# Every third low part of U on GpSimd, and 56 gather steps beside the early keys instead of 44

## The chip, the core and the metric

The kernel runs on one core of a Trainium2 chip. Five engines work side by side, each through its own list of instructions in order: TensorE (PE; matrix products, with its weight loads shown as PEld), VectorE (DVE), ScalarE (ACT), GpSimd (POOL) and SyncE (SP, which here only issues DMAs). They wait for each other through semaphores. The metric is the time of one execution on the device, in microseconds (us). Shorter is better.

## The reference

One transformer layer on 512 tokens of width 2048, in float32. It has a mixer (an mLSTM and a forgetting attention, both behind gates), an attention to a memory of 256 rows, and a feed-forward part called PEER; a residual and a layer norm follow each. Only PEER matters here:

```python
sc = einsum('bshpd,hpnd->bshpn', q, sub_keys)        # scores against 2 x 128 keys, 8 heads
top_s, top_i = top_k(sc, 16)                         # of each half
cand = top_s[..., 0, :, None] + top_s[..., 1, None, :]
best_s, best_pos = top_k(cand, 16)                   # 16 of 256 pairs
g = softmax(best_s)                                  # idx: expert number = key0 * 128 + key1
a = einsum('tkd,td->tk', expert_u[idx], x)           # 128 chosen experts per token
out = einsum('tk,tkd->td', gelu(a) * g, expert_v[idx])
```

There are 16384 experts, rows of the tables U and V of 2048 numbers each.

## The kernel before

Every product of the kernel is made to near float32 precision out of three products of rounded parts: a weight block `raw` of 128 x 1024 is loaded by SP, ScalarE writes its rounded high part `whi` (line 134, in `split`), and the low part `wlo`, the rest, is a subtraction: on VectorE (line 137) or, when `split` is called with `pool=True`, on GpSimd (line 136). `load_w` does this for one block; it counts blocks in `work["n"]` and gives every `work["share"]`-th one's low part to GpSimd, none where `share` is 0. Up to the end of the PEER selection `share` is 8; from there on it is 0. `load_w` also keeps in `work["last"]` the last low part that VectorE made.

PEER is computed in two ways. For 288 of the 512 tokens it is dense: TensorE multiplies these tokens with all of U (`stage_a`, one key of 128 experts at a time, two blocks of 128 x 1024 each, called half keys here: 24 matmuls per block), ScalarE takes the gelu (line 1275), the result is multiplied by gates that are zero where an expert was not chosen (`stage_h`, line 1305), split again into `hph` and `hpl`, and multiplied with V (`stage_o`). For the others, the first block of 128 tokens and 64 + 32 tokens of the last block, the chosen rows are gathered: GpSimd issues an indirect DMA of 128 rows (`gather_rows`, line 885; 1 MB each), and VectorE uses them, for U with a dot product (line 913), for V with a multiply-add (line 916). A gather and its use are one step of a generator (`gathered`). Gathered rows have three buffers, and a gather as well as its use waits for `work["last"]`, which paces it. The last block's generators are called `jobs` and have 194 steps.

The stretch that the change touches goes so. First the selection: `select` finds the top 16 for two heads at a time on VectorE (lines 791 to 828), with two kinds of products on GpSimd (`cand`, line 812, and `eq`, line 827); it ends with the two reductions `sel_i` (line 828). The last block is selected first, since its gathers wait for it, then the two blocks that are dense. Then the gates: for 48 tokens at a time, TensorE transposes what was selected (line 1225), VectorE builds one-hot matrices (`o1`, line 1234, and `o0`, line 1240), TensorE multiplies them (line 1242), ScalarE copies the product to `stage` (line 1245) and its queue writes it to memory as `gd` (line 1247). Then `stage_a` for the first `LOOK` = 76 keys, with `EARLY` = 44 steps of `jobs` spread over them. Their gelus are parked in memory (`gad`, line 1277). Then the main loop: V in groups of 8 keys, four column groups each, with the remaining keys of U and the remaining steps of `jobs` in between; `fetch` reads `gd` back (line 1287) and `gad` (line 1291) through the SP queue.

This is the order in the program text. The order on each engine is made by the tile framework when the program is built: it walks a timeline of estimated costs and issues what comes first, so that keys of U, selection and gate building are interleaved, and any change of an operation's engine moves the order of all engines behind it. Once built, it is fixed.

Buffers of the weight blocks come in two rings that take turns: `W` with 3 raw, 2 high and 2 low buffers, and `E` with 3 of each.

Of the kernel before, what the change touches and what calls it, by code (L numbers as in the profile page):

```python
# [46 lines left out]
def build(tc, I, out):  # L47
    nc = tc.nc
    with ExitStack() as ctx:
# [94 lines left out]
        def load_raw(src, n=1024):  # L144
# [7 lines left out]
        work = {"jobs": None, "rate": 0.0, "due": 0.0, "n": 0, "share": 0, "last": None, "hold": False,  # L152
                "quiet": 0, "normed": None}
# [1099 lines left out]
        acc = mn.tile([P, NK, NDENSE], F32, tag="acc", name="acc")  # L1253

        LOOK = 76
        EARLY = 44
        GA_N = 3
        J = 8
        gas, hs, gates = {}, {}, [None]
# [3 lines left out]
        def stage_a(c):  # L1263

            bank = sm_bank()[:, :NDENSE]
            for kt in range(2):
                uh, ul = load_w(I["uT"][c, kt])
                todo = []
                for kk in range(8):
                    sl = slice(kk * P, (kk + 1) * P)  # L1270
                    xh, xl = X2[kt * 8 + kk]
                    todo.append((bank, uh[:, sl], ul[:, sl], xh[:, :NDENSE], xl[:, :NDENSE], kt * 8 + kk, True))
                products(todo, 0, 15)
            ga = gap.tile([P, NDENSE], F32, tag="ga", bufs=GA_N, name=nm("ga"))
            nc.scalar.activation(ga, bank, AF.Gelu)
            if c in spilled:
                nc.scalar.dma_start(gad[c], ga)
            else:
                gas[c] = ga
# [79 lines left out]
        ahead = [min(NC_, LOOK + -(-c * (NC_ - LOOK) // (NC_ - J))) for c in range(NC_)]  # L1359
        spilled = {a for c in range(NC_) for a in range(ahead[c - 1] if c else 0, ahead[c]) if a - c >= GA_N - 1}  # L1360
        njobs, done = sum(2 * n + 1 for _, n in GATHERED), 0
        for a in range(ahead[0]):
            stage_a(a)
            while done * LOOK < a * EARLY:
                next(jobs, None)
                done += 1

        turn_g = [0]
        for c0 in range(0, NC_, J):
            def fill(i, c0=c0):  # L1370
                if i % 2:
                    c = c0 + i // 2
                    while turn_g[0] < njobs - EARLY and turn_g[0] * (NC_ - 16) <= c * (njobs - EARLY):
                        next(jobs, None)
# [82 lines left out]
```

## Time and profile before

| | |
|---|---|
| median of 3 runs | 4901.81 us (4898.5 to 4901.84) |
| the profiled execution | 4913.27 us, span 4911.5 us |
| TensorE busy | 4713.5 us, 96% of the span |
| VectorE | 3736.2 us, 76% |
| ScalarE | 2127.7 us, 43% |
| GpSimd | 1351.3 us, 28% |

The profile is of one execution. A group of instructions is named by its line, engine, operation and the tiles it writes and reads (`wlo<-raw,whi`). Windows give each engine's busy time between two times of the span, with the clock that TensorE was granted (1.00 is full speed). A row of the waits names the waiting engine and line, then who ended the wait. Matmuls overlap, so their mean durations add up to more than their time.

### The profile page before, as it was taken

The numbers are of one execution on the slowest core, as the hardware profiler recorded it, in microseconds if no ns is written. First come the engines' busy times: TensorE is split into PE (matmuls) and PEld (weight loads), VectorE is DVE, ScalarE is ACT, GpSimd is POOL, SyncE is SP. The second block draws the span as 40 slices with busy tenths as digits, with TensorE's granted clock in tenths as the row PEclk, the third lists the DMA queues.
The fourth block names the chain that finished last, engine by engine and source line by source line (L and its number), as shares of the span: only waits on it lengthen the run. The fifth ranks groups of instructions, "written<-read, shape, count | busy, mean of one in ns | idle before, by whom it ended". The sixth has DMA issues, their size and how long they took to land. (4 is left out here: it accounts for less than half of the span.)

```text
span 4911.5 us, 75235 instructions
## 1 busy us (share of the span) xinstructions
PE 4713.5 (96%) x28705; PEld 4353.5 (89%) x28705; DVE 3736.2 (76%) x5363; ACT 2127.7 (43%) x3106; POOL 1351.3 (28%) x1055
## 2 busy tenths in 40 slices
PE   7999999999999999999999999999998999999997
PEld 6888788878888899999988779999998999999997
DVE  7765666665688776888768585899876878888886
ACT  6665666555543322343332334434443433343333
POOL 1122222311124443334444232332001222221211
PEclk9999999999999999999999999999999999999999
DMA  7888898866559899988889575678778999999994
GB/s 249 283 273 282 302 318 311 276 227 207 190 186 356 328 358 341 339 332 328 303 304 379 201 283 171 215 263 278 277 283 320 346 348 342 344 335 349 359 345 146
DMA packets 380027, 1433.60 MB, mean 292 GB/s; under 512 B 43853, under 2 KB 104909, under 8 KB 320625
## 3 DMA queue, kind: packets, MB, share of 16 engines
q1 hardware_dynamic: 266208, 831.34, 48.5%
q0 software_dynamic: 91712, 559.45, 30.4%
q10 hardware_dynamic: 21744, 38.02, 2.1%
q8 instruction: 224, 3.67, 0.3%
q14 instruction: 139, 1.13, 0.1%
HBM read 1339.13 MB, written 89.40 MB: 291 GB/s over the span
## 5 line engine op out<-in xcount | busy, mean ns | idle before, releaser
L134 ACT CAST whi<-raw 128x1024 fp32r<-128x1024 f32 x1472 | 1526.1, 1051 | 1775.3 <-PE mm L208 814.5
L137 DVE TENSOR_TENSOR wlo<-raw,whi 128x1024 fp32r<-128x1024 f32 x1352 | 1695.5, 1265 | 751.8 <-ACT whi L134 556.0
L885 POOL DMA_INDIRECT rows<-in_peer_v,eid x224 | 379.6, 1695 | 815.0 <-DVE xacc L916 431.4
L885 POOL DMA_INDIRECT rows<-in_peer_u,eid x224 | 322.2, 1438 | 1009.4 <-DVE rows L913 357.8
L208 PE MATMUL po<-hph,whi 128*128 128x288 f32 x2048 | 554.3, 298 | 27.8 <-ACT hph L134 16.9
L913 DVE SCALAR_TENSOR_TENSOR rows<-rows,xacc 128x2048 f32<-128x2048 f32 x224 | 525.7, 2351 | 64.2 <-DMA rows<-in_peer_u,eid 63.4
L916 DVE SCALAR_TENSOR_TENSOR xacc<-rows,dots,xacc 128x2048 f32<-128x2048 f32 x224 | 542.0, 2420 | 40.2 <-DMA rows<-in_peer_v,eid 38.9
L208 PE MATMUL sm<-Ch,whi 128*128 128x288 f32 x2048 | 562.2, 299 | 3.5 <-ACT whi L134 2.5
L208 PE MATMUL sm<-Cl,whi 128*128 128x288 f32 x2048 | 560.7, 298 | 0.0
L208 PE MATMUL po<-hpl,whi 128*128 128x288 f32 x2048 | 553.8, 297 | 1.8 <-DVE hpl L137 1.8
L136 POOL TENSOR_TENSOR wlo<-raw,whi 128x1024 fp32r<-128x1024 f32 x120 | 307.9, 2566 | 699.3 <-ACT whi L134 335.7
L208 PE MATMUL mm<-xh,whi 128*128 128x384 f32 x1280 | 437.3, 344 | 8.0 <-ACT whi L134 2.8
L208 PE MATMUL mm<-xl,whi 128*128 128x384 f32 x1280 | 429.4, 337 | 0.0
L208 PEld LDWEIGHTS po<-hph,whi 128*128 128x128 f32 x2048 | 386.0, 190 | 30.6 <-ACT hph L134 17.2
L208 PEld LDWEIGHTS sm<-Ch,whi 128*128 128x128 f32 x2048 | 386.8, 189 | 5.5 <-ACT whi L134 3.0
L208 PEld LDWEIGHTS po<-hpl,whi 128*128 128x128 f32 x2048 | 386.1, 190 | 2.8 <-DVE hpl L137 2.0
L208 PEld LDWEIGHTS sm<-Cl,whi 128*128 128x128 f32 x2048 | 387.2, 189 | 0.0
L208 PE MATMUL po<-hph,wlo 128*128 128x288 f32 x2048 | 340.9, 297 | 1.4 <-DVE wlo L137 1.3
L208 PE MATMUL sm<-Ch,wlo 128*128 128x288 f32 x2048 | 319.2, 297 | 3.1 <-DVE wlo L137 3.1
L208 PEld LDWEIGHTS po<-hph,wlo 128*128 128x128 f32 x2048 | 296.4, 189 | 5.1 <-DVE wlo L137 2.6
L208 PEld LDWEIGHTS sm<-Ch,wlo 128*128 128x128 f32 x2048 | 287.8, 189 | 5.9 <-DVE wlo L137 4.2
L208 PEld LDWEIGHTS mm<-xh,whi 128*128 128x128 f32 x1280 | 241.4, 189 | 16.1 <-issue 4.1
(430 smaller groups left out, 8833.6 us busy)
## 6 DMA issues: line engine op xcount, KB each, us to landing
raw<-in_w_in SPq DMA_DIRECT2D x512, 512.0 KB, 5.6
raw<-in_uT SPq DMA_DIRECT2D x256, 512.0 KB, 5.1
raw<-in_vq SPq DMA_DIRECT2D x256, 512.0 KB, 6.4
raw<-in_w_xkv SPq DMA_DIRECT2D x64, 512.0 KB, 5.3
raw<-in_w_br_ml SPq DMA_DIRECT2D x64, 512.0 KB, 5.2
raw<-in_w_br_fx SPq DMA_DIRECT2D x64, 512.0 KB, 5.8
raw<-in_w_out SPq DMA_DIRECT2D x64, 512.0 KB, 4.4
raw<-in_peer_wq SPq DMA_DIRECT2D x64, 512.0 KB, 3.4
```

What stands on the lines that cost most here:

```text
L134: nc.scalar.copy(hi, src)
L136: return nc.gpsimd.tensor_sub(lo, src, hi.bitcast(F32))
L137: return nc.vector.tensor_sub(lo, src, hi.bitcast(F32))
L208: nc.tensor.matmul(o, w if stat else x, x if stat else w, start=k == first and x is xh and not part, stop=k == last and part == 1)
L885: i = nc.gpsimd.indirect_dma_start(out=rows, out_offset=None, in_=I[table], in_offset=bass.IndirectOffsetOnAxis(ap=ei[:, k:k + 1], axis=0))
L913: after(nc.vector.scalar_tensor_tensor(rows, rows, 1.0, xacc, op0=ALU.mult, op1=ALU.mult, accum_out=dots[:, k:k + 1]), last())
L916: after(nc.vector.scalar_tensor_tensor(xacc, rows, dots[:, k:k + 1], xacc, op0=ALU.mult, op1=ALU.add), last())
```

## The change

While the first `LOOK` keys of U are run ahead, `work["share"]` is 3: every third low part of U is subtracted by GpSimd instead of VectorE, 50 in the whole program. After them it is 0 again, as it was. And `EARLY` is 56: of the 194 gather steps of the last block, 56 are spread over these keys and 138 are left for the main loop, where it was 44 and 150. Nothing else is edited, and the computed values do not depend on it; the order that is built from it differs on all engines.

```diff
-        EARLY = 44
+        EARLY = 56
...
+        work["share"] = 3
         for a in range(ahead[0]):
             stage_a(a)
             while done * LOOK < a * EARLY:
                 next(jobs, None)
                 done += 1
+        work["share"] = 0
```

## The prediction

> **What bounds the kernel now.** I read the busy shares first, then the stage of the change in windows, then who TensorE waited for, and last the prices of the operations that move. The page's first line:
>
> ```profile
> PE 4713.5 (96%) x28705; PEld 4353.5 (89%) x28705; DVE 3736.2 (76%) x5363; ACT 2127.7 (43%) x3106; POOL 1351.3 (28%) x1055
> ```
>
> TensorE is the bound over the whole span; the change acts only after 3105 us. To place the stages I took the first and last starts (the last two times of each row) of three kinds of matmul: products of U (`sm`), gate-building products (`po<-o,o`), products with V (`po<-hph`).
>
> ```profile
> L208 PE MATMUL sm<-Ch,whi x2048: 289/295/445, 3105.1 to 4813.3; 128*128 128x288 f32 x187
> L1242 PE MATMUL po<-o,o x576: 270/275/547, 3368.0 to 3672.3; 128*128 128x128 f32 x192
> L208 PE MATMUL po<-hph,whi x2048: 288/294/607, 3697.7 to 4882.6; 128*128 128x288 f32 x187
> ```
>
> So: U alone from 3105, U and gate building from 3368, a gap, and the main loop from 3698. Those stages by windows (columns: PE, PEld, DVE, ACT, POOL busy with their instructions, granted clock, DMA share, GB/s):
>
> ```profile
> 3105.00:3368.00 263.00, 251.74 (x1874) 250.33 (x1874) 257.98 (x651) 106.93 (x129) 86.44 (x63) 0.99 0.76 262
> 3368.00:3681.00 313.00, 310.95 (x2408) 310.33 (x2408) 260.56 (x485) 146.92 (x402) 27.34 (x22) 0.99 0.79 280
> 3681.00:3698.00 17.00, 0.29 (x1) 0.29 (x2) 5.39 (x9) 1.19 (x4) 0.94 (x1) 0.63 1.01 356
> 3698.00:3703.00 5.00, 5.00 (x23) 5.00 (x23) 3.33 (x9) 2.68 (x6) 0.00 (x0) 0.54 0.63 179
> 3800.00:3900.00 100.00, 100.00 (x757) 100.00 (x756) 79.18 (x89) 40.37 (x47) 26.05 (x15) 1.00 0.94 355
> 3900.00:4800.00 900.00, 885.23 (x6555) 873.75 (x6555) 747.06 (x842) 339.59 (x428) 204.63 (x129) 0.99 0.92 343
> ```
>
> In the first window VectorE is busy 258.0 of 263 us: it, not TensorE, decides when gate building can begin. In the second TensorE is busy 311.0 of 313 and VectorE has 52.4 us free. The third is a hole of 17 us, the fourth its echo: 0.54 of the clock for 5 us, 2.3 us lost. In the main loop TensorE is full again: 757 matmuls of 288 columns in 100 us, 132.1 ns each, so one half key (24 matmuls, one block of U) costs 3.17 us.
>
> Who TensorE waited for, up to 3600 us (three rows) and after (two; total, times, longest):
>
> ```profile
> PE po L1225 <- DVE sel_i L828: 4.2, 1, 4.2
> PE po L1242 <- DVE o L1240: 3.9, 1, 3.9
> PE sm L208 <- DVE wlo L137: 2.4, 2, 2.1
> ```
> ```profile
> PE po L208 <- ACT hph L134: 16.9, 1, 16.9
> PE po L208 <- ACT whi L134: 10.7, 6, 2.0
> ```
>
> The first three say the same as the window: TensorE stands three times for a VectorE that is behind. The 16.9 us are the hole. Its chain, from the timeline:
>
> ```profile
> 3672.92 0.45 ACT L1245 COPY stage<-po 128x128 f32<-128x128 f32 x2
> 3673.32 2.32 ACTq L1247 DMA_DIRECT2D gd<-stage  x3
> 3683.81 0.62 SPq L1287 DMA_DIRECT2D G<-gd  x1
> 3696.73 0.83 DVE L1305 TENSOR_TENSOR ga<-ga,G 128x288 f32<-128x288 f32 x2 [3.54 <-DMA G<-gd]
> 3697.22 0.80 ACT L134 CAST hph<-ga 128x288 fp32r<-128x288 f32 x2 [12.68 <-DVE ga L1305]
> ```
>
> Last gate matrix copied, written to memory, read back by the SP queue, multiplied, split: 25.4 us from the last gate product (3672.3) to the first V product (3697.7). TensorE ran out of U 8.7 us into it.
>
> **What the change does to the order.** The program's order on each engine is fixed when it is built, so it can be counted in both kernels. Half keys of U standing ahead of an instruction in TensorE's order, and VectorE's and GpSimd's instructions up to the first gate product:
>
> ```
>                                          before   after
> TensorE: first gate transpose (L1225)      44.1    33.3  half keys
>          first gate product (L1242)        77.9    64.9
>          last gate product                151.4   137.2
>          first V product                  154.0   152.0
> VectorE, third sel_i pair to first L1234: wlo 79 -> 45, L913 22 -> 23, the rest equal
> GpSimd, to the last eq: low parts of U 0 -> 22; in the whole program 0 -> 50
> ACT: a gelu that waits for TensorE, ahead of the cast TensorE needs next, main loop: 6 -> 4
> ```
>
> Of the 34 low parts fewer, 22 are on GpSimd and 12 are not yet due, because gate building was moved 13 half keys forward. That settles which sums matter: when VectorE lets the first gate product go, and what TensorE has left behind it.
>
> **The prices.** VectorE's two operations, in 3100 to 3400 us (the first two rows, with the two GpSimd operations of that stretch) and in 3400 to 3600 us, where GpSimd computes nothing (the last two; busy and mean ns of one):
>
> ```profile
> L137 DVE TENSOR_TENSOR wlo<-raw,whi 128x1024 fp32r<-128x1024 f32 x86 | 114.9, 1337 | 5.1 <-PE mm L208 2.9 <-ACT whi L134 2.2
> L913 DVE SCALAR_TENSOR_TENSOR rows<-rows,xacc 128x2048 f32<-128x2048 f32 x25 | 60.8, 2431 | 2.7 <-DMA rows<-in_peer_u,eid 2.7
> L827 POOL TENSOR_TENSOR eq<-eq,ixf 128x512 f32<-128x512 f32 x18 | 38.3, 2146 | 45.5 <-DVE eq L826 45.5
> L812 POOL TENSOR_TENSOR cand<-v 128x512 f32<-128x512 f32 x9 | 13.7, 1521 | 25.6 <-DVE v L795 25.5
> ```
> ```profile
> L137 DVE TENSOR_TENSOR wlo<-raw,whi 128x1024 fp32r<-128x1024 f32 x50 | 60.9, 1220 | 20.6 <-ACT whi L134 19.8 <-PE sm L208 0.6
> L913 DVE SCALAR_TENSOR_TENSOR rows<-rows,xacc 128x2048 f32<-128x2048 f32 x14 | 31.9, 2282 | 1.4 <-DMA rows<-in_peer_u,eid 1.3
> ```
>
> A low part frees 1.22 us of VectorE; a gather's use costs 2.28. But beside GpSimd's work the same operations are longer, 1337 and 2431 ns: 86 x 0.117 + 25 x 0.149 = 13.8 us. A collision in the timeline, the minimum/median/maximum of the GpSimd operations, and the low parts on both engines before 1480 us:
>
> ```profile
> 3193.67 4.92 POOL L827 TENSOR_TENSOR eq<-eq,ixf 128x512 f32<-128x512 f32 x2 [3.40 <-DVE eq L826]
> 3194.57 2.86 DVE L913 SCALAR_TENSOR_TENSOR rows<-rows,xacc 128x2048 f32<-128x2048 f32 x1
> 3197.35 2.31 DVE L137 TENSOR_TENSOR wlo<-raw,whi 128x1024 fp32r<-128x1024 f32 x1
> ```
> ```profile
> L827 POOL TENSOR_TENSOR eq<-eq,ixf x32: 1278/2126/3788, 1374.1 to 3357.8; 128x512 f32<-128x512 f32 x32
> L812 POOL TENSOR_TENSOR cand<-v x16: 1046/1060/2827, 1363.8 to 3341.9; 128x512 f32<-128x512 f32 x16
> L136 POOL TENSOR_TENSOR wlo<-raw,whi x120: 2357/2404/4452, 35.2 to 3093.6; 128x1024 fp32r<-128x1024 f32 x120
>   PEld ma L208: 5.4, 6
> ```
> ```profile
> L137 DVE TENSOR_TENSOR wlo<-raw,whi 128x1024 fp32r<-128x1024 f32 x546 | 702.4, 1300 | 372.1 <-ACT whi L134 287.4 <-PE mm L208 41.6 <-PE ma L208 23.0
> L136 POOL TENSOR_TENSOR wlo<-raw,whi 128x1024 fp32r<-128x1024 f32 x78 | 195.3, 2504 | 565.7 <-ACT whi L134 317.9 <-PE mm L208 114.3 <-PE ma L208 70.4
> ```
>
> What a low part on GpSimd takes back from VectorE, from both sides: before 1480 us, where VectorE is less loaded, 546 x 0.080 us / 78 = 0.56 us each. In the stretch itself 13.8 us over 18 x 1.28 + 9 x 1.05 = 32.5 us of undisturbed GpSimd time, 0.42 per us, times 2.40 us: 1.02. By the one collision, 0.58 + 1.09 us over 2.56: 0.65 per us, 1.57. I take 1.2, between the two of the stretch, because VectorE there is never idle and feels each collision; 0.56 and 1.57 stay as ends.
>
> The Trainium skill (SBUF — State Buffer, Who interferes with whom) has a rule against this change: a VectorE instruction with two SBUF inputs and a GpSimd instruction that reads SBUF exclude each other, and the later one blocks for the whole of the other. The collision agrees with it; by the rule's worst case every low part takes its full 2.40 us back, and the sum below would end at +37 us in place of +11.
>
> **The sum.** Against the profiled execution (span 4911.5, its own time 4913.27); it is 11.5 us above the median of 4901.81, to which I apply the difference.
>
> - VectorE to the first gate product: -34 x 1.22 + 1 x 2.28 + 22 x 1.2 = -12.8 us.
> - TensorE behind it: 178.1 -> 191.1 half keys of U, 13 x 3.17 = +41.2. The gate products are the same.
> - The hole: 14.8 half keys, 47 us, now stand behind the last gate product and cover the 25.4 us chain: -16.9, and -2.3 of slow clock. Nothing is late next unless the read-back exceeds 47.
> - Main loop: two whi waits fewer at 10.7 / 6 = 1.8: -3.6.
> - GpSimd in order: VectorE waits for eq and cand behind low parts; the stretch has 2.9 us of it on 27, I take as much again, +3; the end is 5 eq pairs with two low parts each just ahead in the new order, 10 x 2.40 = +24. TensorE's weight loads waited 5.4 us for 120 low parts of GpSimd: 50 cost +2.
>
> ```profile
> DVE sel_i L828 <- POOL eq L827: 1.8, 3, 0.7
> DVE b L791 <- POOL cand L812: 1.1, 2, 0.7
> ```
>
> At nothing: the other low parts and the extra gather uses beside gate building. Between first and last gate product VectorE loses 25 low parts (-30.5) and gains 5 uses (+11.4) and 24 collisions (+28.8): +10 against 52.4 us free; with that cover gone, +10. The 12 gathers move 12 MB forward, where the DMA share is 0.76 to 0.79; the main loop at 0.92 is relieved, but no wait there names a gather, so 0, at best -5. The pace of a gather names the last low part on VectorE, so it is released no later than before; 12 more issues stand among GpSimd's low parts.
>
> Total -12.8 + 41.2 - 19.2 - 3.6 + 5 = +10.6: 4912.4 us, a gain in the hole paid back by VectorE's start of gate building.
>
> **Rivals.**
> - Faster: collisions cost 0.56, as before 1480 us. Then the first term is -26.9 and the total -3.5, without the waits for GpSimd -8.5; with -5 in the main loop 4888. It decides below 0.6 us a low part with GpSimd never in the way. For it: the hole surely closes. Against: the fuller stretch shows 1.02.
> - GpSimd becomes the queue that decides: a low part behind a gather that waits for a row buffer, an eq behind two low parts. Price 24 us on VectorE in place of 3: 4933. It decides once each of the five pairs is waited for. Against: GpSimd is busy 86 of 263 us, and 22 x 2.40 = 53 more leave room.
> - They cancel (0.8 to 1.0 us a collision): 4903 to 4908. That the change does not take place is excluded by the order.
>
> **Chances.** Forecast 0.44 (its own range 4902 to 4922), faster 0.23, GpSimd's queue 0.20, cancelled 0.13. The mark of 0.2%, 9.8 us, is about what a measurement of this kernel can tell from no change; half of the forecast lies below it. So faster 0.23, same 0.34, slower 0.43. The range runs from 0.56 with relief to the queue rival: 4886 to 4938.
>
> **What would show it.** Right: the hole at the first V product gone; gate building starting 5 to 20 us earlier than 3368, not 40; TensorE standing 35 to 50 us for VectorE up to there (10.5 before, 41.2 of U less, 8 of time won); L137 means above 1337 ns up to there. Wrong: gate building near 3330 (collisions cheap), or TensorE waiting for GpSimd's low parts.

## The result, and the profile after

The changed kernel takes 4937.25 us, the median of 6 runs (4931.07 to 4941.42), against 4898.38 us of 6 runs of the kernel before on the same chip: a ratio of 1.0067, 95% interval 1.0057 to 1.0078. It is slower by 0.57 to 0.78%, on the side given and just inside the range given (4886 to 4938), but by about three times the forecast of +10.6 us. The profiled execution has a span of 4939.7 us, 28.2 more than the 4911.5 before. The medians lie 38.9 us apart: the execution profiled before took 14.9 us more than that kernel's median, the one after 4.2 more. The stages below divide the 28.2 us; some 10 us stand in no stage.

The page's first line of the kernel after: TensorE does the same work, VectorE is busy longer though it runs 50 instructions fewer.

```profile
PE 4714.6 (95%) x28705; PEld 4352.8 (88%) x28705; DVE 3761.0 (76%) x5313; ACT 2125.4 (43%) x3106; POOL 1501.8 (30%) x1105
```

The first and last starts (last two times of a row) of U products, gate-building products and V products after:

```profile
L208 PE MATMUL sm<-Ch,whi x2048: 289/295/606, 3103.8 to 4841.5; 128*128 128x288 f32 x187
L1242 PE MATMUL po<-o,o x576: 270/275/582, 3367.0 to 3688.6; 128*128 128x128 f32 x192
L208 PE MATMUL po<-hph,whi x2048: 288/294/442, 3737.7 to 4910.8; 128*128 128x288 f32 x187
```

From these marks come four stages: *selection* (first U product to first gate product), *gates* (to the last gate product), *chain* (to the first V product) and *loop* (to the end). The forecast by stage is the prediction's own terms, laid where they fall: 1.2 half keys of U fewer in the gates, 14.8 in the chain against 25.4 us, two more in the loop.

| stage, us | before | after | difference | forecast |
|---|---|---|---|---|
| up to the first U product | 3105.1 | 3103.8 | -1.3 | 0 |
| selection | 262.9 | 263.2 | +0.3 | -9.8 (-12.8 and +3) |
| gates | 304.3 | 321.6 | +17.3 | -3.8 |
| chain | 25.4 | 49.0 | +23.6 | +21.5 |
| loop | 1213.7 | 1202.0 | -11.7 | +0.4 |
| sum | 4911.5 | 4939.7 | +28.2 | +8.3, and +2 in no one stage (0.3 is lost in rounding) |

The windows of the first three stages after (columns as in the prediction):

```profile
3104.00:3367.00 263.00, 222.71 (x1561) 219.43 (x1561) 258.00 (x620) 89.35 (x107) 127.18 (x84) 0.92 0.67 238
3367.00:3689.00 322.00, 304.62 (x2319) 301.36 (x2320) 286.89 (x468) 142.46 (x395) 106.34 (x52) 0.98 0.77 278
3689.00:3738.00 49.00, 47.36 (x358) 47.13 (x357) 28.43 (x30) 19.14 (x31) 16.05 (x9) 1.00 1.01 386
```

The hole is gone: 47.4 of 49 us busy where TensorE stood for 17. It stands elsewhere: 40.3 us in the selection, at 0.92 of the clock, where it was 11.3 us at 0.99, and 17.4 us in the gates, where it was 2. Whom it waited for between 3050 and 3720 us (first fence) and behind that (second):

```profile
PE sm L208 <- DVE wlo L137: 22.9, 8, 8.0
PE po L1242 <- DVE o L1240: 17.8, 12, 2.6
PE po L1225 <- DVE sel_i L828: 10.6, 1, 10.6
...
PE sm L208 <- POOL wlo L136: 0.5, 1, 0.5
```
```profile
PE po L208 <- ACT whi L134: 6.3, 4, 2.0
```

The three waits for VectorE come to 51.3 us; in the same stretch of the kernel before they came to 12.3 (10.5 of it up to 3600 us). For GpSimd's own low parts it waits 0.5 us.

**What a low part on GpSimd costs VectorE.** Groups of the selection (count, then busy and mean ns of one), before and after:

```profile
L137 DVE TENSOR_TENSOR wlo<-raw,whi 128x1024 fp32r<-128x1024 f32 x76 | 102.8, 1353 | 0.0
L913 DVE SCALAR_TENSOR_TENSOR rows<-rows,xacc 128x2048 f32<-128x2048 f32 x22 | 53.9, 2452 | 2.0 <-DMA rows<-in_peer_u,eid 2.0
L807 DVE CAST ixf<-ix 128x64 f32<-128x64 uint32 x9 | 1.6, 175 | 0.0
L818 DVE TENSOR_SCALAR pi<-pos 128x32 uint32<-128x32 uint32 x9 | 1.5, 170 | 0.0
```
```profile
L137 DVE TENSOR_TENSOR wlo<-raw,whi 128x1024 fp32r<-128x1024 f32 x43 | 74.3, 1730 | 0.5 <-ACT whi L134 0.5
L913 DVE SCALAR_TENSOR_TENSOR rows<-rows,xacc 128x2048 f32<-128x2048 f32 x23 | 66.6, 2897 | 3.3 <-DMA rows<-in_peer_u,eid 3.3
L136 POOL TENSOR_TENSOR wlo<-raw,whi 128x1024 fp32r<-128x1024 f32 x20 | 51.7, 2599 | 10.7 <-ACT whi L134 7.4 <-PE sm L208 3.2
L807 DVE CAST ixf<-ix 128x64 f32<-128x64 uint32 x9 | 8.3, 922 | 0.2
L818 DVE TENSOR_SCALAR pi<-pos 128x32 uint32<-128x32 uint32 x9 | 6.5, 721 | 0.0
```

Above the undisturbed 1220 and 2282 ns, after loses 43 x 0.510 + 23 x 0.615 = 36.1 us on the two large operations and 11.7 us on two tiny ones; before it lost 76 x 0.133 + 22 x 0.170 = 13.9. The difference, 33.9 us over 20 low parts, is 1.7 us each, where the prediction took 1.2 and its upper end was 1.57. A subtraction moved to GpSimd frees 1.22 us of VectorE and takes more than that back. VectorE also stands 6.2 us for ScalarE's copies of the scores (line 1198) at the start of the stretch, 2.0 before. In the timeline of that stretch (start, duration), VectorE and GpSimd:

```profile
3184.23 4.30 DVE L913 SCALAR_TENSOR_TENSOR rows<-rows,xacc 128x2048 f32<-128x2048 f32 x1
...
3190.20 6.02 DVE L137 TENSOR_TENSOR wlo<-raw,whi 128x1024 fp32r<-128x1024 f32 x1
```
```profile
3183.48 2.90 POOL L136 TENSOR_TENSOR wlo<-raw,whi 128x1024 fp32r<-128x1024 f32 x1
...
3190.26 2.54 POOL L827 TENSOR_TENSOR eq<-eq,ixf 128x512 f32<-128x512 f32 x2
3192.74 2.40 POOL L136 TENSOR_TENSOR wlo<-raw,whi 128x1024 fp32r<-128x1024 f32 x1
```

The gather's use ends 2.15 us after GpSimd's low part, its own 2.28 us but for a little: it did nothing beside it. The subtraction at 3190.20 ends 1.08 us after three GpSimd operations in a row: it waited for all three and then took its 1.2 us. The Trainium skill (SBUF — State Buffer, Who interferes with whom) says that two such instructions exclude each other for the whole of one; these rows agree.

**The gates.** Groups of that stage, before and after:

```profile
L137 DVE TENSOR_TENSOR wlo<-raw,whi 128x1024 fp32r<-128x1024 f32 x75 | 91.3, 1220 | 35.0 <-ACT whi L134 33.5 <-ACT stage L1245 0.7 <-PE sm L208 0.6
L1240 DVE TENSOR_SCALAR o<-iota,i0T,gT 128x128 f32<-128x128 f32 x287 | 84.0, 346 | 8.9 <-PE po L1242 8.6
```
```profile
L1240 DVE TENSOR_SCALAR o<-iota,i0T,gT 128x128 f32<-128x128 f32 x287 | 131.2, 512 | 13.3 <-PE po L1242 13.1
L136 POOL TENSOR_TENSOR wlo<-raw,whi 128x1024 fp32r<-128x1024 f32 x25 | 67.0, 2685 | 51.3 <-ACT whi L134 37.0 <-PE sm L208 9.4 <-ACT stage L1245 3.1
L913 DVE SCALAR_TENSOR_TENSOR rows<-rows,xacc 128x2048 f32<-128x2048 f32 x28 | 64.0, 2284 | 7.0 <-DMA rows<-in_peer_u,eid 6.8
L137 DVE TENSOR_TENSOR wlo<-raw,whi 128x1024 fp32r<-128x1024 f32 x49 | 59.8, 1220 | 13.9 <-ACT whi L134 13.3 <-issue 0.5
```

Here it isn't the large operations that suffer (1220 and 2284 ns, as without GpSimd) but the one-hot matrices, small operations with one tile as input: 346 to 512 ns, 47.2 us of busy time in all, 1.9 us for each of 25 low parts. VectorE still has 35 us free in the window, but the two engines go hand in hand: VectorE waits 13.1 us for TensorE to free a one-hot matrix's buffer, and TensorE 17.8 us, in 12 waits, for the next matrix. So free time elsewhere doesn't cover. Four one-hot matrices without a low part, then four with one, and that low part:

```profile
3392.15 1.10 DVE L1240 TENSOR_SCALAR o<-iota,i0T,gT 128x128 f32<-128x128 f32 x4
```
```profile
3397.64 3.40 DVE L1240 TENSOR_SCALAR o<-iota,i0T,gT 128x128 f32<-128x128 f32 x4
```
```profile
3398.55 2.40 POOL L136 TENSOR_TENSOR wlo<-raw,whi 128x1024 fp32r<-128x1024 f32 x1
```

2.30 us more, nearly the whole of the low part.

### The profile page after: what moved, and what is told of

Read it like the earlier page. It is cut to its first block, busy times and chain, and to the rows that moved or that the text cites. A ratio compares the mean times of both kernels' runs of the same rounds, so it can differ in the third digit from the quotient of the medians.

```text
span 4939.7 us, 75256 instructions
## 1 busy us (share of the span) xinstructions
PE 4714.6 (95%) x28705; PEld 4352.8 (88%) x28705; DVE 3761.0 (76%) x5313; ACT 2125.4 (43%) x3106; POOL 1501.8 (30%) x1105
## 3 DMA queue, kind: packets, MB, share of 16 engines
q1 hardware_dynamic: 266208, 831.34, 47.4%
## 5 line engine op out<-in xcount | busy, mean ns | idle before, releaser
L137 DVE TENSOR_TENSOR wlo<-raw,whi 128x1024 fp32r<-128x1024 f32 x1302 | 1652.3, 1280 | 736.1 <-ACT whi L134 539.2
L136 POOL TENSOR_TENSOR wlo<-raw,whi 128x1024 fp32r<-128x1024 f32 x170 | 442.2, 2604 | 774.0 <-ACT whi L134 404.4
L885 POOL DMA_INDIRECT rows<-in_peer_v,eid x224 | 411.7, 1838 | 839.2 <-DVE wlo L137 393.6
L916 DVE SCALAR_TENSOR_TENSOR xacc<-rows,dots,xacc 128x2048 f32<-128x2048 f32 x224 | 540.4, 2412 | 40.3 <-DMA rows<-in_peer_v,eid 38.8
```

The costliest lines, as they stand in the source:

```text
L136: return nc.gpsimd.tensor_sub(lo, src, hi.bitcast(F32))
L137: return nc.vector.tensor_sub(lo, src, hi.bitcast(F32))
L885: i = nc.gpsimd.indirect_dma_start(out=rows, out_offset=None, in_=I[table], in_offset=bass.IndirectOffsetOnAxis(ap=ei[:, k:k + 1], axis=0))
L916: after(nc.vector.scalar_tensor_tensor(xacc, rows, dots[:, k:k + 1], xacc, op0=ALU.mult, op1=ALU.add), last())
```

## The experiments

The theory after the result: a low part on GpSimd and an operation of VectorE on the same on-chip memory keep each other out. The rivals: GpSimd's occupied queue delays what stands behind it; the built order, with gate building 13 half keys of U earlier, is at fault by itself; the gathers moved beside the keys are what costs. Stages of the profiled execution of each kernel (the first U product starts between 3092.7 and 3107.8 in all, though no edit reaches work ahead of it, so a single profile is worth some us; stages are counted from that start). The kernel before was profiled in an execution slower than any of its six, 56 gathers alone in the fastest of its ten, so these two may differ by some us for that alone. The last column is against the kernel before, in the same session.

| kernel | selection | gates | chain | loop | ratio, 95% interval |
|---|---|---|---|---|---|
| before | 262.9 | 304.3 | 25.4 | 1213.7 | 1 |
| after | 263.2 | 321.6 | 49.0 | 1202.0 | 1.0067 [1.0057, 1.0078] |
| share alone | 243.8 | 300.4 | 60.3 | 1216.9 | 1.0040 [1.0026, 1.0054] |
| 56 gathers alone | 284.8 | 306.8 | 15.0 | 1196.3 | 1.0012 [0.9998, 1.0026] |
| after, fill for the low part | 225.6 | 303.2 | 48.0 | 1200.4 | 0.9951 [0.9934, 0.9967] |
| after, three fills | 229.4 | 304.7 | 45.6 | 1200.3 | 0.9970 [0.9960, 0.9981] |
| share only from key 38 | 261.2 | 306.0 | 29.2 | 1211.1 | 1.0004 [0.9992, 1.0015] |
| 84 keys, 48 gathers | 267.0 | 300.7 | 46.6 | 1167.9 | 0.9955 [0.9939, 0.9971] |
| 80 keys, 48 gathers | 268.2 | 305.2 | 28.2 | 1183.9 | 0.9955 [0.9944, 0.9966] |
| 84 keys, 62 gathers | 286.0 | 320.9 | 35.1 | 1142.2 | 0.9980 [0.9967, 0.9993] |
| 92 keys, 68 gathers | 287.1 | 329.9 | 80.6 | 1097.4 | 0.9984 [0.9974, 0.9994] |
| 84 keys, 62 gathers from key 24 | 196.2 | 377.6 | 77.1 | 1140.4 | 0.9991 [0.9978, 1.0004] |
| 84 keys, 48 gathers from key 24 | 191.0 | 334.5 | 100.1 | 1170.1 | 0.9983 [0.9969, 0.9998] |

### The two parts, one at a time

Share alone, against the kernel after:

```diff
-        EARLY = 56
+        EARLY = 44
```

> Every third low part of U on GpSimd, but 44 gather steps as before. The built order brings gate building forward as in the full change: first gate product after 64.8 half keys of U, last after 133.3. Theory 1, the low parts collide with VectorE and give back nothing: VectorE still reaches the first gate product near 3360 us, TensorE stands some 35 to 45 us for it up to there, and the time stays 15 to 35 us above the kernel before. Theory 2, the 12 extra gather uses are what makes the change slower: the time falls to or below that of before, by 0 to 20 us.

56 gathers alone, against the kernel before:

```diff
-        EARLY = 44
+        EARLY = 56
```

> 56 gather steps instead of 44, all low parts of these keys on VectorE as before. The built order has the first gate product after 81.6 half keys and the last one right before the first V product (154.0), so nothing covers the read-back of the gates. Theory 1: the order knows of these uses, TensorE stands for VectorE no more than before (about 10 us up to the first gate product), the hole grows from 17 to about 25 us, and the time is 0 to 12 us above before. Theory 2: the uses alone cost what the full change costs, 25 us or more.

Measured: 4923.19 and 4905.85 us, beside 4904.65 of the kernel before. The share costs 0.40%; the gathers alone cost nothing that can be told from no change. The two don't simply add up: the full change costs 0.67%, and its interval lies above that of the share alone, so beside the share the 12 gathers do cost. The second has a better loop (-17.4 us) and pays it back in the selection (+21.9, of it 3.7 half keys or 11.7 us of U that its order puts there). In the first the order of gate building is as early as in the kernel after, and VectorE lets it go 19.4 us earlier than there: it has 18 uses of gathers in that stage (50.8 us) in place of 23 (66.6). The added gathers are why the selection after didn't become shorter at all.

### The same order without the reading

Against the kernel after, GpSimd's low parts of these keys are replaced by a fill, which reads nothing and is shorter, in the same place:

```diff
-                return nc.gpsimd.tensor_sub(lo, src, hi.bitcast(F32))
+                return nc.gpsimd.memset(lo.bitcast(F32), 0.0) if work["share"] == 3 else nc.gpsimd.tensor_sub(lo, src, hi.bitcast(F32))
```

> The full change, but the 50 low parts that GpSimd makes are filled with zeros by it in place of the subtraction (so this part of the computation is left out): GpSimd writes the same tiles and reads nothing. The built order is nearly that of the full change (first gate product after 65.1 half keys, last after 137.2, first V product after 152). Theory 1, collisions: VectorE reaches the first gate product at 3325 to 3338 us, TensorE stands less than 15 us for it up to there, L137 falls back towards 1.22 us, and the time is 15 to 30 us below before. Theory 3, the order itself (gates too early, GpSimd's queue in the way) costs the time whatever GpSimd reads: the time stays within 10 us of the full change.

Then three fills behind the cast, so that GpSimd is held at least as long as by the subtraction:

```diff
-            nc.scalar.copy(hi, src)
+            cast = nc.scalar.copy(hi, src)
...
-                return nc.gpsimd.tensor_sub(lo, src, hi.bitcast(F32))
+                return [(m := nc.gpsimd.memset(lo.bitcast(F32), 0.0), after(m, cast)) for _ in range(3)][-1][0] if work["share"] == 3 else nc.gpsimd.tensor_sub(lo, src, hi.bitcast(F32))
```

> The full change, but each of the 50 low parts on GpSimd is replaced by three fills of the same tile with zeros behind the cast of its high part (this part of the computation is left out), so that GpSimd is held about as long as by the subtraction (3 x 0.97 us by the run with one fill, 2.6 by the subtraction) and waits for the same cast, but reads nothing. The built order is nearly that of the full change (first gate product after 64.3 half keys, last after 137.9). Theory 1, collisions of reads: VectorE reaches the first gate product at 3322 to 3338 us as with one fill, and the time is 15 to 30 us below before. Theory of the queue, GpSimd's time in front of eq, cand and the gathers is what VectorE and TensorE wait for: the first gate product comes at 3355 us or later, and the time is above before.

Both leave out these 50 low parts (the values are zeros). The built order is all but that of the kernel after: the first gate product stands behind 65.1 and 64.3 half keys of U, 64.9 there. Measured: 4878.88 us beside 4904.65, and 4885.07 beside 4902.73. Against the profile after, the one fill takes 60.8 us off, of it 37.6 in the selection and 18.4 in the gates, the two stages that hold the low parts. Their groups, one fill, in the selection:

```profile
L137 DVE TENSOR_TENSOR wlo<-raw,whi 128x1024 fp32r<-128x1024 f32 x43 | 57.1, 1327 | 1.7 <-ACT whi L134 1.7
L913 DVE SCALAR_TENSOR_TENSOR rows<-rows,xacc 128x2048 f32<-128x2048 f32 x23 | 55.2, 2401 | 1.5 <-DMA rows<-in_peer_u,eid 1.3
```

and three fills, first the selection, then the gates:

```profile
L136 POOL MEMSET wlo<- 128x1024 f32 x60 | 57.0, 957 | 25.0 <-ACT whi L134 23.1 <-PE sm L208 0.8
L137 DVE TENSOR_TENSOR wlo<-raw,whi 128x1024 fp32r<-128x1024 f32 x42 | 55.0, 1312 | 2.5 <-ACT whi L134 2.5
```
```profile
L1240 DVE TENSOR_SCALAR o<-iota,i0T,gT 128x128 f32<-128x128 f32 x288 | 105.7, 500 | 17.2 <-PE po L1242 16.9
L136 POOL MEMSET wlo<- 128x1024 f32 x75 | 73.1, 980 | 34.8 <-ACT whi L134 22.6 <-ACT stage L1245 7.8 <-PE sm L208 1.5
```

Three fills hold GpSimd 57.0 us in the selection, more than the 51.7 of the subtractions, and VectorE's subtraction takes 1312 ns in place of 1730. So the queue theory falls, and so does the one of the order: with this order and a GpSimd that is as busy, but reads nothing, the kernel is faster than before. What costs is that GpSimd reads while VectorE works. In the gates the fills too lengthen the one-hot matrices, but less: the group is busy 105.7 us, 21.7 more than before, where the subtractions made it 47.2 more (the mean of 500 ns hides this, since these records overlap). TensorE waits 4.3 us for them there, after the change 17.8. So the reading isn't all of it in the gates.

### The share only beside the gates

If the selection is where VectorE has no time to lose, the share may pay behind it. Against the kernel before:

```diff
-            stage_a(a)
+            work["share"] = 3 if a >= 38 else 0; stage_a(a)
...
-        turn_g = [0]
+        work["share"] = 0; turn_g = [0]
```

> Every third low part of U on GpSimd only from key 38 on, that is beside gate building and not beside the selection; 76 keys and 44 gather steps as before. The built order is that of before up to the first gate product (after 76.8 half keys, 77.9 before), and the last gate product stands 9.2 half keys (29 us) ahead of the first V product. Theory 1, VectorE's load in the selection is what a low part on GpSimd fails to relieve: the first gate product comes where it came before (3360 to 3372 us), TensorE stands no more for it than before (about 10 us), the mean of L1240 rises above 450 ns by collisions, which cost TensorE at most 10 us in this stretch, the hole is gone, and the time falls by 8 to 20 us. If collisions beside gate building are what costs, TensorE stands 15 us or more for L1240 there and the time is at or above before.

Measured: 4906.21 us beside 4905.02. This was a miss. Its selection is that of the kernel before and its hole is gone, but TensorE waits for the one-hot matrices. The row of its waits (3050 to 3730 us), and the group in its gates:

```profile
PE po L1242 <- DVE o L1240: 19.3, 13, 5.8
```
```profile
L1240 DVE TENSOR_SCALAR o<-iota,i0T,gT 128x128 f32<-128x128 f32 x287 | 124.1, 483 | 18.0 <-PE po L1242 17.5
```

The gain in the hole and the loss in the gates are of one size: 16.9 us against 19.3. Free time of VectorE in that window buys nothing while the small operations are made just before they are needed. The one-hot matrices have four buffers (`o0`) in all these runs; more were not tried.

### Closing the hole without GpSimd

The hole was there because TensorE ran out of U. More keys ahead, with the gathers in the same pace, close it too. Against the kernel before, with 84 and with 80 keys:

```diff
-        LOOK = 76
-        EARLY = 44
+        LOOK = 84
+        EARLY = 48
```

> The kernel before with 84 keys of U run ahead instead of 76 and 48 gather steps beside them, no low part on GpSimd there. The built order has 14.1 half keys of U between the last gate product and the first V product (2.6 before). If the hole of 17 us and its slow clock are worth what the sum took, the hole is gone and the time falls by 15 to 25 us, to 4874 to 4885; if the first V products wait anyway for something else, it stays within 8 us of before.

```diff
-        LOOK = 76
-        EARLY = 44
+        LOOK = 80
+        EARLY = 48
```

> The kernel before with 80 keys ahead and 48 gather steps: in the built order the first gate product stands after 79.1 half keys, 8.6 half keys (27 us) lie between the last gate product and the first V product, and two gelus stand ahead of a needed cast in the main loop (four with 84 keys and 48 steps, six before). If the hole and these waits are what is left to win: the hole is covered, just, the main loop loses 8 to 14 us of stands and slow clock against before, and the time is at that of 84 keys or up to 8 us below, 4872 to 4884. If the waits of the main loop were of no weight, it is 4880 to 4888.

Measured: 4883.31 us beside 4904.65 and 4884.29 beside 4907.55, both 0.9955 of the kernel before and the fastest kernels here that compute everything. The rows of 84 keys: its waits up to 3730 us, and the window of its chain.

```profile
PE po L1225 <- DVE sel_i L828: 5.2, 1, 5.2
PE sm L208 <- DVE wlo L137: 1.9, 1, 1.9
...
PE po L1242 <- DVE o L1240: 0.7, 1, 0.7
```
```profile
3669.00:3716.00 47.00, 45.95 (x345) 45.48 (x345) 32.56 (x41) 21.41 (x35) 6.41 (x4) 1.00 1.02 381
```

TensorE runs 14 half keys more ahead of V, 14 x 3.17 = 44.4 us, in 21.7 us more (614.3 against 592.6), and the loop is 45.8 us shorter. The one-hot matrices take 344 ns there, as before.

### More gathers, or later ones, beside more keys

Each against the kernel before; the loop's waits become fewer with fewer gathers left, so more of them were moved:

```diff
-        LOOK = 76
-        EARLY = 44
+        LOOK = 84
+        EARLY = 62
```

> The kernel before with 84 keys of U ahead instead of 76 and 62 gather steps beside them instead of 44, no low part on GpSimd there. The built order has 9.9 half keys of U (31 us) between the last gate product and the first V product, and one gelu ahead of a needed cast in the main loop (six before). If the hole and the waits of the main loop add up: the hole goes (-17 to -20 us) and the main loop loses 10 to 17 us, while the first gate product comes 5 to 10 us later: 4868 to 4882. If moving gather steps forward only moves their cost, the time stays at that of 84 keys and 48 steps, 4880 to 4888.

```diff
-        LOOK = 76
-        EARLY = 44
+        LOOK = 92
+        EARLY = 68
```

> The same with 92 keys and 68 steps: 23.9 half keys between the last gate product and the first V product, one gelu ahead of a needed cast. The read-back takes 25 us and is covered by 31 us already, so more keys ahead should give nothing more: within 6 us of the kernel with 84 keys and 62 steps. A loss of more than 8 us would say that parking more of the gelus in memory costs something that I have not counted.

Measured: 4890.99 and 4894.79 us beside 4902.73. Faster than before, but less than with 48. With 84 keys the 14 more gathers take 25.7 us off the loop, 11.5 off the chain and cost 19.0 in the selection and 20.2 in the gates. So, with 84 keys, the steps were begun only at key 24, past most of the selection, with 62 and with 48 steps:

```diff
-            while done * LOOK < a * EARLY:
+            while done * (LOOK - 24) < (a - 24) * EARLY:
```

> 84 keys ahead and 62 gather steps as in the run before, but the steps begin at key 24, so that most of them stand beside gate building and few beside the selection; no low part on GpSimd there. In the built order VectorE has 5 uses in place of 22 before the first gate product (after 59.5 half keys) and 46 beside gate building. If what costs is VectorE's load in the selection alone: TensorE no longer stands 10 to 20 us up to the first gate product, the main loop keeps its gain, and the time is 10 to 20 us below that of 84 keys with 48 steps, 4863 to 4875. If VectorE's load beside gate building costs as well (by its durations it would be busy some 345 of 357 us there): TensorE stands 10 us or more for L1240 and the time is 4880 or above.

> The same with 48 steps from key 24 on: 3 uses before the first gate product, 33 beside gate building (some 308 of 338 us of VectorE). First theory: 5 to 10 us below 84 keys with 48 steps spread evenly, 4873 to 4880, with TensorE's stands before the first gate product gone. Second: no better than it.

Measured: 4898.33 and 4897.41 us beside 4902.61. The first of the two returns values that are not numbers, for a reason left open, so it is shown for its time alone. Against 84 keys with 48 gathers in an even pace, the selection is 71 and 76 us shorter, and gates and chain together are 107 and 87 us longer; the loop is 28 us shorter in the first and 2 longer in the second. The waits of the first up to 3730 us, and of the second behind 3740:

```profile
PE po L1242 <- DVE o L1240: 22.1, 10, 4.3
PE sm L208 <- ACT ga L1275: 10.1, 3, 7.1
```
```profile
PE po L208 <- ACT whi L134: 7.7, 5, 1.9
PE po L208 <- DVE wlo L137: 6.4, 10, 2.2
PE sm L208 <- DVE wlo L137: 4.6, 6, 2.5
```

What the gathers no longer take beside the selection they take beside the gates and in the loop. All four are misses: the place of the gathers moves the cost, and of the losses worked on in these runs without GpSimd only the hole was taken away for good.

## Why the prediction was right, and where it was not

- **The number: right in its side, and inside the range by luck.** 4937.25 us is past the forecast's own range (4902 to 4922) and 0.75 us below the end of the whole range, which came from the rival of GpSimd's queue (4933); that rival is not what happened. Nor is the +37 us of a full 2.40 us a low part, near as it is to the medians' difference: a low part took 1.7 back in the selection, and the loss in the gates stood at nothing in that sum.
- **The hole gone, V behind its chain: right.** -16.9 us forecast, 1.6 us of standing left; the chain stage +23.6 against +21.5.
- **A gain paid back by VectorE's start of gate building: right in kind.** Gate building was to start 5 to 20 us earlier, and started 1 us earlier. TensorE stood 40.3 us up to there (35 to 50 given), the mean of the subtraction is 1730 ns (above 1337 given), and the queue rival is refuted by 0.5 us of waits for GpSimd's low parts and by the three fills.
- **The price of a collision, "I take 1.2": mis-sized.** It measured 1.7 us by VectorE's groups, and (263.2 - 225.6) / 22 = 1.7 by the fills; the first gate product came at 3367.0, not at 3355. The term of -12.8 us became +0.3. Of these 13.1 us, the collisions are 7.5 (33.9 against 22 x 1.2), VectorE's longer wait for the scores 4.2, and its wait for gathered rows 1.3. Of the three rows that bounded the price, the single collision (1.57) was nearest. The mean over the stretch (1.02) perhaps came out low because only part of GpSimd's time met a VectorE operation that could be held; no run shows it. The price also left out the small operations, a third of the loss on the large ones.
- **"At nothing" for the collisions beside gate building: the step that failed.** +10 us with that cover gone was its price; the stage gave +17.3 where -3.8 was forecast. The 52.4 us free were an average over the window, while the one-hot matrices are made just before TensorE needs them; and the collisions fall on these, at 1.9 us a low part. The share from key 38 shows it alone: 19.3 us of waits with the selection untouched.
- **The loop, -3.6 us and gathers "at 0, at best -5": too small.** It is 11.7 us shorter with two half keys (6.3 us) more in it, 18 us in all, and the gathers alone give 17.4. The windows of the loop, before and after, and of 56 gathers alone:

```profile
3698.00:4911.00 1213.00, 1170.05 (x8656) 1155.75 (x8655) 973.69 (x1136) 452.64 (x574) 264.87 (x163) 0.98 0.87 323
```
```profile
3738.00:4939.00 1201.00, 1166.92 (x8703) 1153.92 (x8702) 957.33 (x1113) 454.49 (x575) 274.48 (x153) 0.99 0.86 319
```
```profile
3700.00:4895.00 1195.00, 1161.91 (x8655) 1149.71 (x8653) 946.71 (x1111) 456.38 (x572) 267.05 (x151) 0.99 0.86 317
```

  TensorE is idle 34 us in place of 43, and its matmuls are faster: 47 more (6.2 us) in 3.1 us less. Of that the prediction had only the 2.3 us behind the hole. Stands of 2 us were counted for themselves alone, but most were followed by a spell at half the clock: besides the one behind the hole, the loop before has four such spells and the loop after has one, some 8 us lost against 2 by the lengths of their matmuls. The better loop goes with the fewer gather steps left in it: 1196 to 1202 us in the four kernels with 76 keys and 138 steps left, 1211 to 1217 in the three with 150.
- **GpSimd in order, +3 and +2: not seen.** VectorE waited 0.8 us for `cand` and for no `eq` in the selection, less than the 2.9 us before, and the weight loads waited 0.7 us for a low part of GpSimd.

So the sum, +10.6 us, was right in its sign with two costs put too low (by 10 us in the selection, 21 in the gates) and one gain put too low (by 12 in the loop).

## What to carry to other kernels

Before work is moved from a full VectorE to GpSimd, set what it frees against what GpSimd's operation takes back while VectorE reads: here 1.22 us against 1.7 to 1.9, so the move lost whatever room GpSimd had. A cost may be covered by free time only if the consumer has a buffer ahead of it; where an engine makes tiles just before the next one needs them, an average of free time covers nothing. If TensorE stands for lack of ready work, look first for more work of its own to run ahead (80 or 84 keys in place of 76, 0.45% faster), before another engine is made faster.

## What the runs showed of the hardware

- Operations with one input tile were held too, and the shortest most of all: the shift of 128 x 32 (line 818) went from a mean of 170 to 721 ns, the cast of 128 x 64 (line 807) from 175 to 922, and the one-hot matrices from 346 to 512. The shift of the same shape right behind (line 819) stayed at 177: what is held is the operation that meets a low part, not every one of its kind. Fills on GpSimd held the one-hot matrices as well (402 ns with one fill, 500 with three; 9.2 and 21.7 us more in all), but hardly the subtraction with two inputs (1312 to 1327 ns, where 1353 was seen before with GpSimd's other products). The Trainium skill (SBUF — State Buffer, Who interferes with whom) makes this difference: two inputs collide only with a GpSimd operation that reads, while copies, casts and operations with a scalar can collide with any; the rows agree.
- One VectorE operation was kept out by several GpSimd operations in a row (6.02 us for a subtraction of 1.2). Beside the gates the subtractions and the gathers' uses were not held (1220 and 2284 ns), and the timeline shows why: all but one of them that ran beside a low part had begun before it, and then the low part was held. There are six such places, with low parts of 2.52 to 3.71 us where 2.40 is undisturbed; in one a use runs from 3447.74 to 3450.02, and the low part begun at 3449.43 takes 2.84. The one use that began behind a low part, at 3502.21, wasn't held either; the two low parts there took 7.17 us. With the share only from key 38, three uses began while a low part ran, and they took 4.51, 2.60 and 3.17 us. Why GpSimd's low parts begin beside one-hot matrices so often no run tested.
- In the loop before, four of the five times that TensorE stood for 1.8 to 2.0 us were followed by 3.4 us or more at half the clock. One of them, in three windows of the kernel before (the stand, the spell behind it, and past it; the third number from the end is the clock):

```profile
4020.00:4026.00 6.00, 4.29 (x33) 4.05 (x31) 2.13 (x1) 1.22 (x2) 0.00 (x0) 1.00 0.99 374
4027.00:4030.00 3.00, 3.00 (x14) 3.00 (x14) 3.00 (x3) 2.08 (x3) 1.10 (x1) 0.50 0.53 163
4031.00:4036.00 5.00, 5.00 (x40) 5.00 (x39) 4.07 (x7) 1.21 (x2) 2.67 (x2) 1.00 0.81 274
```

  14 matmuls in 3 us, where 23 fit: 1.1 us lost in this window alone, by a stand of 2.0 us.
